# Two token tiles to an accumulator bank, weights loaded a job ahead, decay rows on ScalarE's queue

## The chip, the cores and the metric

The kernel runs on one core of a Trainium2 chip. The metric is the time of one execution on the device in microseconds (us), the median of several runs. A core has five engines with a queue of instructions each, worked through in order: TensorE (PE, matrix multiplications into PSUM banks), VectorE (DVE), ScalarE (ACT), GpSimd (POOL) and SyncE (SP, which here only starts transfers). ACT also starts transfers. PSUM banks of 128 x 512 floats hold what PE has summed until ACT or DVE has read it.

## What is computed

One decoder layer over 1024 tokens of width 1024 with two branches: differential attention (8 heads) and a Mamba-2 scan (8 groups of 4 heads). Cut to what matters:

```python
h = rmsnorm(x, g_pre)
q, k, v, g_att, z, xbc, dt_raw, merge_logits = jnp.split(h @ w_in, SPLIT_IDX, axis=-1)
# attention: two softmax maps for each head, a = p0 - lam * p1, causal, with a bias by distance
o = rmsnorm(diff_attention(q, k, v, rel_bias, lam), att_subln_g) * (1.0 - lambda_init)
y_att = (o * silu(g_att)) @ w_att_proj
# scan: depthwise convolution over 4 tokens, then chunks of tokens with a running state
xs, Bm, Cm = split(silu(causal_depthwise_conv(xbc, conv_w, conv_b)))
dt = softplus(dt_raw + dt_bias)
a_cs = cumsum(dt * -exp(a_log))                    # within a chunk
y_diag = einsum((Cm . Bm) * tril(exp(a_cs[l] - a_cs[s])), xs * dt)
y_off = einsum(Cm, state) * exp(a_cs)
state = state * exp(a_cs[-1]) + einsum(Bm, exp(a_cs[-1] - a_cs), xs * dt)
y = group_rmsnorm((y_diag + y_off + d_skip * xs) * silu(z), ssm_norm_g, 8)
y_ssm = y @ w_ssm_proj
mixed = sigmoid(gate_att) * y_att + sigmoid(gate_ssm) * y_ssm
x = x + rmsnorm(mixed @ w_out, g_post)
```

## The kernel before

All projections are split: an operand is a rounded high part plus a low part, and a product is three matmuls (`mm3`, L153). A weight arrives by a transfer on SP's queue (`load_cols`, L143) in a buffer `raw`, ACT rounds it (L97) and POOL or DVE subtracts (L98). Of `raw` there are three buffers, so SP's next load waits until a split is done.

The stages, in order of time: the **head** squares, scales and transposes x (`ptx`, L386) into hT as high and low parts (`hTH` L388 on ACT, `hTL` L389 on DVE); **attention** runs 8 heads; `pya` projects its output; the **groups** of the scan, eight of them with eight chunks each; the **final projections** `pys` (of the scan's output) and `pout`. For half of the tokens, `pys` is begun early within the last group (`pye`, read at L889).

A `Stream` holds jobs: keys, queries, values (`pv`) and a merge gate for a head; in a group four convolution channels b, c, x0, x1 (`pub`, `puc`, `pux`) and the gate z (`pz`). A job is a load and steps of 12 matmuls of 512 columns or 24 of 256. Between the score blocks of attention and the chunks of the scan a number of steps is taken. `pv` and `pz` have the tokens on the partitions: a tile of 128 tokens gives 128 x 256 in a bank of its own. All these go through two PSUM banks (`psp`). ACT takes a tanh of the bank (`sz`, L706), then DVE multiplies with the bank (L707); a convolution is read twice by ACT (L725, L726), then come three taps on DVE (L728), a tanh on ACT (L729) and a product on DVE (L730).

A chunk needs a tile `mt` of decays: the row of a_cs for 4 heads, broadcast to 128 partitions by a transfer from DRAM (`mt<-arow_d`, SP's queue, L752, four buffers, three chunks ahead), then four Relu and an Exp on ACT (L783, L784) and a product with `cbm` on DVE (L785). `prepare` (L755) makes the transposes `px`, copied by ACT into `xb` (L768); `advance` (L787) has the matmuls `pd` that use `mt` and the state, and `finish` (L817) norms four chunks, transposes (`pty`) and stores `yT` (L829, L830) in DRAM as y_d, from where `yT_l` comes back (L963) as the operand of `pys`.

PE's order is that of the code (`manual_schedule`, L251). The order on ACT, DVE, POOL and SP is made by a scheduler from the program order and the priorities (`high_priority`) that some instructions carry.

Of the kernel before, what the change touches and what calls it, by code (L numbers as in the profile page):

```python
# [46 lines left out]
AHEAD = 2000  # L47
# [27 lines left out]
def tile_hybrid_layer(ctx: ExitStack, tc: tile.TileContext, x, g_pre, w_in, lq1, lk1, lq2, lk2,  # L75
# [56 lines left out]
    def load_cols(w, row0, col0, width, tag, name, off=0, wh=None, wl=None, eng=None):  # L132
# [4 lines left out]
        for c in range(0, width - off, P):  # L137
            n = min(P, width - off - c)
            cols = slice(off + c, off + c + n)
            for k0 in range(0, KT, 4):  # L140
                raw = wts.tile([P, 4, P], F32, tag="raw", bufs=3, name=f"{name}r{off + c}_{k0}")
                r0 = row0 + k0 * P
                nc.sync.dma_start(raw[:, :, 0:n], w[r0:r0 + 4 * P, col0 + c:col0 + c + n].rearrange("(k p) c -> p k c", p=P))  # L143
                split(wh[:, k0:k0 + 4, cols], wl[:, k0:k0 + 4, cols], raw[:, :, 0:n], eng)
# [26 lines left out]
    def proj_N(w, t, n, name):  # L171

        wh, wl = w
        ps = psp.tile([P, 512], F32, tag="pp", name=name)
        sl = slice(t * P, (t + 1) * P)
        mm3(ps[:, 0:n], [((hTH[:, k, sl], hTL[:, k, sl]), (wh[:, k, 0:n], wl[:, k, 0:n])) for k in range(KT)])
        return ps

    class Stream:
# [5 lines left out]
        def add(self, load, steps):  # L185
            self.jobs.append([load, steps, None])

        def load(self, i):
            if i < len(self.jobs) and self.jobs[i][2] is None:
                self.jobs[i][2] = self.jobs[i][0]()  # L190

        def advance(self):

            if self.at is None:
                for i in range(self.ahead + 1):
                    self.load(self.done + i)
                self.at = self.jobs[self.done][1](self.jobs[self.done][2])
            try:
                next(self.at)
                return True  # L200
# [50 lines left out]
    pe_scope.enter_context(tc.manual_schedule(engines={mybir.EngineType.PE}))  # L251
# [10 lines left out]
    class Head:  # L262
# [15 lines left out]
        def keys(self, w, half):  # L278
# [3 lines left out]
            with tc.high_priority(offset=AHEAD):  # L282
                nc.scalar.activation(kh[lo, 0, sl], ps[lo], AF.Copy)
                nc.scalar.activation(kh[hi, 1, sl], ps[hi], AF.Copy)
                nc.vector.tensor_tensor(kl[lo, 0, sl], ps[lo], f32(kh[lo, 0, sl]), op=ALU.subtract)
                nc.vector.tensor_tensor(kl[hi, 1, sl], ps[hi], f32(kh[hi, 1, sl]), op=ALU.subtract)
            for part in (kh, kl):
                nc.scalar.dma_start(f32(part[hi, 0, sl]), f32(part[lo, 0, sl]))
                nc.scalar.dma_start(f32(part[lo, 1, sl]), f32(part[hi, 1, sl]))
            yield  # L290

        def queries(self, w, half):
# [3 lines left out]
            with tc.high_priority(offset=AHEAD):  # L296
                nc.scalar.activation(qs[lo, 0, sl], ps[lo], AF.Copy, scale=DK ** -0.5)
                nc.scalar.activation(qs[hi, 1, sl], ps[hi], AF.Copy, scale=DK ** -0.5)
                nc.vector.scalar_tensor_tensor(qs[hi, 0, sl], ps[lo], DK ** -0.5, f32(qs[lo, 0, sl]), op0=ALU.mult, op1=ALU.subtract)
                nc.vector.scalar_tensor_tensor(qs[lo, 1, sl], ps[hi], DK ** -0.5, f32(qs[hi, 1, sl]), op0=ALU.mult, op1=ALU.subtract)  # L300
            yield

        def load_values(self):
            wh = wts.tile([P, KT, 288], F32R, tag="wbh", bufs=1, name=f"wvh{self.h}")
            wl = wts.tile([P, KT, 288], F32R, tag="wbl", bufs=1, name=f"wvl{self.h}")
            load_cols(w_in, 0, OV + self.h * P, P, "", f"wv{self.h}", wh=wh, wl=wl, eng=nc.gpsimd)
            load_cols(w_in, 0, OG + self.h * P, 2 * P, "", f"wg{self.h}", off=P, wh=wh, wl=wl, eng=nc.gpsimd)
            return wh, wl

        def values(self, w):  # L310
            vv, gg = self.vv, self.gg
            for t in range(NT):
                ps = proj_N(w, t, 256, f"pv{self.h}_{t}")
                with tc.high_priority(offset=AHEAD):
                    nc.scalar.activation(vv[:, t, 0:DV], ps[:, 0:DV], AF.Copy)
# [767 lines left out]
```

## Time and profile before

| | |
|---|---|
| median of three runs | 1950.76 us (1948.28 to 1950.99) |
| the profiled execution | 1953.8 us, of which the span is 1951.9 |
| mean granted clock of PE | 0.978 |
| transfers | 175.64 MB, mean 90 GB/s |
| SP's wait at L752 for PE's pd | 264.0 us, 38 times, longest 15.5 |
| the chain that ended last | PE 35%, DVE 8%, DMA 6% (5% of it mt<-arow_d), ACT 3% |

A row of a timeline begins with the start and the duration in us, then the engine, the line, the operation, what it writes and what it reads, how often, and in brackets how long the engine had been idle and what ended that. In lists of waits the numbers are total, count and longest. A group of instructions of the same kind is given as total busy time and mean of one. Time at which an engine that holds nobody up is idle costs nothing.

### The profile page before, as it was taken

The numbers are of one execution on the slowest core, as the hardware profiler recorded it, in microseconds if no ns is written. First come the engines' busy times: TensorE is split into PE (matmuls) and PEld (weight loads), VectorE is DVE, ScalarE is ACT, GpSimd is POOL, SyncE is SP. The second block draws the span as 40 slices with busy tenths as digits, with TensorE's granted clock in tenths as the row PEclk, the third lists the DMA queues.
The fourth block names the chain that finished last, engine by engine and source line by source line (L and its number), as shares of the span: only waits on it lengthen the run. The fifth ranks groups of instructions, "written<-read, shape, count | busy, mean of one in ns | idle before, by whom it ended". The sixth has DMA issues, their size and how long they took to land.

```text
span 1951.9 us, 27895 instructions
## 1 busy us (share of the span) xinstructions
PE 1830.9 (94%) x10249; PEld 1579.8 (81%) x10249; DVE 1159.9 (59%) x2564; ACT 858.7 (44%) x2143; POOL 473.6 (24%) x388
## 2 busy tenths in 40 slices
PE   4999999999999999999989899999999988798998
PEld 3888988889889888888778787888888876576886
DVE  4265665655656553126756759686867778564333
ACT  5345454555545443115544446455544455242211
POOL 2212111121111112212422314142332325341210
PEclk9999999999999999999999999999999998898999
DMA  5322122131221126422222223232322234674422
GB/s 164 87 55 79 36 82 58 49 84 39 73 63 44 58 73 208 150 75 63 65 55 76 65 72 91 55 91 56 82 61 74 75 95 152 206 239 132 157 83 79
DMA packets 225734, 175.64 MB, mean 90 GB/s; under 512 B 13116, under 2 KB 187550, under 8 KB 225598
## 3 DMA queue, kind: packets, MB, share of 16 engines
q1 hardware_dynamic: 193660, 116.48, 21.8%
q10 hardware_dynamic: 31938, 57.38, 8.8%
q8 instruction: 81, 1.33, 0.3%
q14 instruction: 55, 0.45, 0.1%
HBM read 133.82 MB, written 33.17 MB: 86 GB/s over the span
## 4 chain that ended last, share of the span: by engine, by line
PE 35%; DVE 8%; DMA 6%; ACT 3%; issue 2%; POOL 1%; SPq 0%; ACTq 0%; DVEq 0%; POOLq 0%
PE pys L153 6%; PE pz L153 6%; DMA mt<-arow_d 5%; PE pout L153 5%; PE puc L153 4%; PE pub L153 4%; PE pux L153 3%; DVE xT L728 3%; PE pd L793 2%; PE pg L153 1%; ACT mt L783 1%; PE pd L796 1%; PE pd L798 1%; DVE rst_y L107 1%; PE pye L153 1%
## 5 line engine op out<-in xcount | busy, mean ns | idle before, releaser
L153 PE MATMUL pz<-wzh,hTH 128*128 128x256 f32 (+1 forms) x512 | 157.2, 307 | 39.5 <-ACT xT L726 21.8
L153 PE MATMUL pz<-wzl,hTH 128*128 128x256 f32 (+1 forms) x512 | 151.4, 296 | 0.0
L153 PE MATMUL pz<-wzh,hTL 128*128 128x256 f32 (+1 forms) x512 | 150.8, 295 | 0.0
L783 ACT ACTIVATE mt<-mt,acs 128x128 f32<-128x128 f32 x256 | 86.5, 392 | 141.7 <-DMA mt<-arow_d 129.5
L153 PE MATMUL pv<-wvl,hTH 128*128 128x256 f32 x512 | 144.5, 282 | 0.0
L153 PE MATMUL pv<-wvh,hTL 128*128 128x256 f32 x512 | 144.2, 282 | 0.0
L153 PE MATMUL pv<-wvh,hTH 128*128 128x256 f32 x512 | 143.4, 280 | 0.0
L153 PEld LDWEIGHTS pz<-wzh,hTH 128*128 128x128 f32 x512 | 103.0, 201 | 46.3 <-ACT xT L726 24.9
L779 POOL TENSOR_TENSOR v<-xb,dsk 128x256 f32<-128x256 f32 x64 | 53.2, 831 | 225.7 <-ACT xb L768 205.1
L153 PEld LDWEIGHTS pz<-wzl,hTH 128*128 128x128 f32 x512 | 103.0, 201 | 0.4
L153 PEld LDWEIGHTS pz<-wzh,hTL 128*128 128x128 f32 x512 | 102.5, 200 | 0.0
L153 PEld LDWEIGHTS pv<-wvh,hTH 128*128 128x128 f32 x512 | 97.2, 190 | 0.6 <-PE pq L153 0.6
L153 PEld LDWEIGHTS pv<-wvl,hTH 128*128 128x128 f32 x512 | 96.7, 189 | 0.0
L153 PEld LDWEIGHTS pv<-wvh,hTL 128*128 128x128 f32 x512 | 96.1, 188 | 0.0
L447 DVE TENSOR_REDUCE ng<-s 128x2 f32<-128x1024 f32 (+2 forms) x96 | 91.5, 954 | 1.8
L728 DVE SCALAR_TENSOR_TENSOR xT<-ux,cw,xT 128x512 f32<-128x512 f32 x96 | 85.2, 887 | 11.8 <-ACT xT L726 11.0
L98 DVE TENSOR_TENSOR al<-pta,ah 128x512 fp32r<-128x512 f32 (+2 forms) x96 | 51.0, 554 | 50.1 <-ACT ah L97 49.0
L458 ACT ACTIVATE p<-s,ngm 128x512 f32<-128x512 f32 (+3 forms) x128 | 76.0, 611 | 7.0 <-DVE ngm L453 6.4
L805 POOL TENSOR_TENSOR st<-st,elast 128x256 f32<-128x256 f32 x48 | 39.1, 815 | 141.1 <-DVE st L806 113.3
L793 PEld LDWEIGHTS pd<-xdt,mt 128*128 128x128 f32 x512 | 65.5, 196 | 8.7 <-DVE mt L785 5.1
L490 PE MATMUL po<-vv,al 128*128 128x256 f32 x288 | 72.2, 284 | 0.0
L793 PE MATMUL pd<-xdt,mt 128*128 128x64 f32 x512 | 66.0, 273 | 6.0 <-DVE mt L785 6.0
(1110 smaller groups left out, 5697.7 us busy)
## 6 DMA issues: line engine op xcount, KB each, us to landing
mt<-arow_d SPq DMA_DIRECT2D x64, 256.0 KB, 5.0
sig_d<-gt ACTq DMA_DIRECT2D x32, 256.0 KB, 2.0
y_d<-yT ACTq DMA_DIRECT2D x32, 256.0 KB, 2.9
yT_l<-y_d SPq DMA_DIRECT2D x24, 256.0 KB, 4.9
kh<-kh ACTq DMA_DIRECT2D x32, 128.0 KB, 2.2
kl<-kl ACTq DMA_DIRECT2D x32, 128.0 KB, 2.6
o_d<-oT ACTq DMA_DIRECT2D x16, 256.0 KB, 2.0
oTl<-o_d SPq DMA_DIRECT2D x8, 512.0 KB, 4.3
```

The costliest lines, as they stand in the source:

```text
L98: (eng or nc.vector).tensor_tensor(l, src, f32(h), op=ALU.subtract)
L107: nc.vector.scalar_tensor_tensor(t, t, -0.5, v, op0=ALU.mult, op1=ALU.mult)
L153: nc.tensor.matmul(ps, a, b, start=(i == 0), stop=(i == n - 1))
L447: nc.vector.tensor_reduce(ng, s[:, :, 0:width], axis=AX.X, op=ALU.max, negate=True)
L458: nc.scalar.activation(self.p[i][:, m, 0:width], s[:, m, 0:width], AF.Exp, bias=neg[:, m:m + 1], accum_out=sums[:, i, m:m + 1])
L490: nc.tensor.matmul(po[:, 0:256], al, vv[:, k, :], start=False, stop=(k == qb))
L728: nc.vector.scalar_tensor_tensor(out_h, u[:, j:j + 512], cw3[:, j, ct:ct + 1], out_h, op0=ALU.mult, op1=ALU.add)
L779: nc.gpsimd.tensor_tensor(v4(self.v), xs, b4(dsk[:, hs]), op=ALU.mult)
L783: nc.scalar.activation(mt[:, i, :], mt[:, i, :], AF.Relu, scale=-1.0, bias=acs[:, c, g.g * HG + i:g.g * HG + i + 1])
L793: nc.tensor.matmul(pd[:, 0, i * PH:(i + 1) * PH], mt[:, i, :], self.xdt[:, i * PH:(i + 1) * PH], start=True, stop=True)
L796: nc.tensor.matmul(pd[:, 1, 256:512], self.xb[:, 256:384], self.xe, start=True, stop=True)
L805: nc.gpsimd.tensor_tensor(v4(new), v4(state), b4(elast[:, c, hs]), op=ALU.mult)
```

## The change

The change keeps every matmul. It removes all priorities and instead delays what is emitted: `post(n, fn)` holds a piece of code back for n steps of the stream, `tick` counts a step and emits what is due, `flush` emits the rest. Splits of loaded weights, multiplications that follow a tanh, taps and tanh of the convolutions and the products of a chunk are posted so.

```diff
+    def post(n, fn):
+
+        item = [now[0] + n, fn]
+        posts.append(item)
+        return item
...
-                raw = wts.tile([P, 4, P], F32, tag="raw", bufs=3, name=f"{name}r{off + c}_{k0}")
...
+                    raw = wts.tile([P, 4, P], F32, tag="raw", bufs=4, name=f"{name}r{off + c}_{i}")
...
-                split(wh[:, k0:k0 + 4, cols], wl[:, k0:k0 + 4, cols], raw[:, :, 0:n], eng)
+                post(after + i, lambda raw=raw, i=i, n=n, cols=cols:
+                     split(wh[:, i * 4:i * 4 + 4, cols], wl[:, i * 4:i * 4 + 4, cols], raw[:, :, 0:n], eng or nc.gpsimd))
```

All jobs of heads and of groups are put in the stream beforehand, so that a job's weights are loaded one job ahead across the border of a head or a group. Values and gates z put two token tiles in a bank (except in the first group):

```diff
+            count = 1 if g == 0 else 2
+            for t in range(0, NT, count):
+                ps = psp.tile([P, 512], F32, tag="pp", name=f"pz{g}_{t}")
...
+                    proj_N(w, t, 256, ps[:, 0:256])
+                    yield
+                    proj_N(w, t + 1, 256, ps[:, 256:512])
+                z = ps[:, 0:256 * count].rearrange("p (t c) -> p t c", t=count)
+                sz = self.sz[:, t:t + count, :]
+                nc.scalar.activation(sz, z, AF.Tanh, scale=0.5)
...
+                    post(1, lambda sz=sz, z=z: nc.vector.scalar_tensor_tensor(sz, sz, 1.0, z, op0=ALU.add, op1=ALU.mult))
```

The load of `mt` goes to ACT's queue, its Relu and Exp get a function of their own that is called before `prepare`, the state's decay goes from POOL to DVE:

```diff
+        def decays(self):
+            g, c, mt = self.group, self.c, self.mt
+            for i in range(HG):
+                nc.scalar.activation(mt[:, i, :], mt[:, i, :], AF.Relu, scale=-1.0, bias=acs[:, c, g.g * HG + i:g.g * HG + i + 1])
+            nc.scalar.activation(mt, mt, AF.Exp, scale=-1.0)
...
-            nc.sync.dma_start(self.mt, bass.AP(arow_d.tensor, arow_d.offset + self.group.g * HG * S + self.c * P,
+            nc.scalar.dma_start(self.mt, bass.AP(arow_d.tensor, arow_d.offset + self.group.g * HG * S + self.c * P,
...
-                        nc.gpsimd.tensor_tensor(v4(new), v4(state), b4(elast[:, c, hs]), op=ALU.mult)
+                    nc.vector.tensor_tensor(v4(new), v4(state), b4(elast[:, c, hs]), op=ALU.mult)
```

In the other direction, the copies of keys and the small transfers th, mx, xr, gpost and mix_d go from ACT's queue to SP's. In the head, ACT squares all eight tiles in a row, DVE does all the scaling, transposes come in pairs and use two banks of the scores besides:

```diff
+        for t in range(NT):
+            squared(t)
+            if t == 3:
+                scaled(0)
+        turned(0, (0, 1))
...
+        turned(0, (6, 7))
+        scaled(1)
```

In attention the sum of the two maps' outputs is one reduction on DVE instead of a copy on ACT and a sum on DVE. In the scan, the z of the last group moves partly behind that group's first chunk, `pye` starts at its third chunk, the loads of w_out only at its fifth, and yT and ys have a buffer less each. Every second of the first eight y loads for `pys` is issued on ACT:

```diff
+            steps = 24 + 4 * (g in (0, 1)) - 4 * (g == SG - 2)
...
+            if (g, c) == (SG - 1, 2):
+                stream.finish(marks[SG])
...
-                nc.sync.dma_start(f32(tl), y_d[i, :, sl])
-                split(th, tl, f32(tl), nc.gpsimd if i % 2 else nc.vector)
+                (nc.scalar if half == 0 and i % 2 else nc.sync).dma_start(f32(tl), y_d[i, :, sl])
+                items.append(post(after, lambda i=i, th=th, tl=tl: split(th, tl, f32(tl), nc.gpsimd if i % 2 else nc.vector)))
```

What this makes of the order, at the places that matter. ACT in the middle of the scan, before, at the border of two groups (`sqy_7` squares the last chunk of the one, `mt_3` belongs to the fourth chunk of the next, L783 is Relu, L784 Exp, `xb` the copy of px; each sz is one token tile):

```order
L814 ACTIVATE sqy_7_12218,ssy_1_11564<-v_7_12012 128x256 [waits DVE_49,Pool_49]
L783 ACTIVATE mt_3_12390<-mt_3_12390,acs 128x128 [waits DMAHW1_49,PE_49]
L783 ACTIVATE mt_3_12390<-mt_3_12390,acs 128x128 x2
L706 ACTIVATE sz_12023<-pz_5_12238 128x256 [waits PE_49]
L783 ACTIVATE mt_3_12390<-mt_3_12390,acs 128x128
L768 ACTIVATE xb_1_12272<-px_1_12267 128x512 [waits PE_49]
L784 ACTIVATE mt_3_12390<-mt_3_12390 128x512 [waits Activation_49]
L706 ACTIVATE sz_12023<-pz_6_12288 128x256 [waits PE_49]
L706 ACTIVATE sz_12023<-pz_7_12315 128x256 [waits PE_49]
```

ACT at the same place after the change:

```order
L863 DMA mt_3_12191<-arow_d 128x4x128 [waits PE_49]
L926 ACTIVATE sqy_7_12062,ssy_1_11379<-v_7_11827 128x256 [waits DVE_49,Pool_49]
L858 ACTIVATE mt_3_12191<-mt_3_12191,acs 128x128 [waits DMAHW2_49]
L858 ACTIVATE mt_3_12191<-mt_3_12191,acs 128x128 x2
L795 ACTIVATE sz_11835<-pz_4_11996 128x512 [waits PE_49]
L878 ACTIVATE xb_1_12090<-px_1_12085 128x512 [waits PE_49]
L858 ACTIVATE mt_3_12191<-mt_3_12191,acs 128x128
L859 ACTIVATE mt_3_12191<-mt_3_12191 128x512 [waits Activation_49]
L795 ACTIVATE sz_11835<-pz_6_12096 128x512 [waits PE_49]
```

The trigger of the load of mt now stands on ACT itself, one instruction ahead of its first Relu, and a sz covers two token tiles.

ACT at the start, before (`sqx` squares a tile of x, `xt` scales one, `hTH` reads a transposed bank):

```order
L374 ACTIVATE sqx_3_151,ssx_144<-xt_113 128x1024 [waits DMAHW6_49,Activation_49]
L374 ACTIVATE sqx_0_228,ssx_227<-xt_118 128x1024 [waits DMAHW7_49,Activation_49]
L379 ACTIVATE xt_109<-xt_109,rsy_x_155 128x1024 [waits DVE_49]
L374 ACTIVATE sqx_1_230,ssx_227<-xt_120 128x1024 [waits DMAHW0_49,Activation_49]
L379 ACTIVATE xt_113<-xt_113,rsy_x_155 128x1024
L374 ACTIVATE sqx_2_232,ssx_227<-xs_qs 128x1024 [waits DMAHW1_49,Activation_49]
L97 ACTIVATE wk0h<-wk0r_0_126 128x512 [waits DMAHW3_49]
L374 ACTIVATE sqx_3_234,ssx_227<-xs_kh 128x1024 [waits DMAHW2_49,Activation_49]
L97 ACTIVATE wk0h<-wk0r_4_130 128x512 [waits DMAHW4_49]
L97 ACTIVATE wq0h<-wq0r_0_136 128x512 [waits DMAHW5_49]
L388 ACTIVATE hTH<-ptx_0_171,gcol 128x512 [waits PE_49]
L388 ACTIVATE hTH<-ptx_1_178,gcol 128x512 [waits PE_49]
```

And after:

```order
L424 ACTIVATE sqx_144,ssx_136<-xt_113 128x1024 [waits DMAHW6_49,Activation_49]
L424 ACTIVATE sqx_164,ssx_137<-xt_118 128x1024 [waits DMAHW7_49,Activation_49]
L424 ACTIVATE sqx_166,ssx_137<-xt_120 128x1024 [waits DMAHW0_49,Activation_49]
L424 ACTIVATE sqx_168,ssx_137<-xs_qs 128x1024 [waits DMAHW1_49,Activation_49]
L434 ACTIVATE hTH<-ptx_0_172,gcol 128x512 [waits PE_49]
L424 ACTIVATE sqx_170,ssx_137<-xs_kh 128x1024 [waits DMAHW2_49,Activation_49]
L434 ACTIVATE hTH<-ptx_1_173,gcol 128x512 [waits PE_49]
L97 ACTIVATE wk0h<-wk0r_0_126 128x512 [waits DMAHW3_49]
L97 ACTIVATE wq0h<-wq0r_0_132 128x512 [waits DMAHW5_49]
L434 ACTIVATE hTH<-ptx_2_190,gcol 128x512 [waits PE_49]
L97 ACTIVATE wk0h<-wk0r_1_128 128x512 [waits DMAHW4_49]
L97 ACTIVATE wq0h<-wq0r_1_134 128x512 [waits DMAHW6_49]
```

The squares of the second half no longer alternate with scalings, and the first hTH stands ahead of the splits of wk0 and of the last square.

SP between the early block and the final projections, after the change (`mix_d<-the` stores an early block, `yT_l<-y_d` loads the scan's output):

```order
L169 DMA wp_0_4r_0_16723<-in_w_ssm_proj 128x4x128 [waits DMAHW4_49,DMAHW1_49,Pool_49]
L1002 DMA mix_d<-the_16561 128x512 [waits DMAHW5_49,DMAHW2_49,DVE_49]
L1180 DMA gpost<-in_g_post 128x1024 [waits DMAHW3_49]
L1098 DMA yT_l_16605<-y_d 128x512 [waits PE_49]
L1098 DMA yT_l_16611<-y_d 128x512
L1098 DMA yT_l_16617<-y_d 128x512 [waits DMAHW0_49]
L1098 DMA yT_l_16623<-y_d 128x512 [waits DMAHW2_49]
L1121 DMA mx_0_16662<-mix_d 128x512 [waits DMAHW4_49,PE_49]
```

The y loads on SP stand behind the store of the last early block; four of the first eight are not here but on ACT's queue.

More of the change, by code (lines that the diff above doesn't have):

```diff
@@ L169, in proj_T, with proj_N @@
         return ps
[L171 removed]
+    def proj_N(w, t, n, ps):
         wh, wl = w
[L174 removed]
         sl = slice(t * P, (t + 1) * P)
[L176 to L177 removed]
+        mm3(ps, [((hTH[:, k, sl], hTL[:, k, sl]), (wh[:, k, 0:n], wl[:, k, 0:n])) for k in range(KT)])
     class Stream:
@@ L849, in tile_hybrid_layer @@
         chunks = [(g, c) for g in range(SG) for c in range(NT)]
-        made, squares = {}, {}
-        def chunk(i):
-            if i not in made:
-                g, c = chunks[i]
-                if c % 4 == 0:
-                    squares[g, c // 4] = small.tile([P, 4], F32, tag="ss4", name=f"ssy{g}_{c // 4}")
-                made[i] = Chunk(groups[g], c, squares[g, c // 4][:, c % 4:c % 4 + 1])
-            return made[i]
         early = []
```

581 lines of the change are left out of this document (339 added, 242 removed).

## The prediction

> **What bounds the kernel now.** I read the page's busy times first, then the windows by stage, then what TensorE (PE) waited for, and only then the queues behind those waits.
>
> ```profile
> PE 1830.9 (94%) x10249; PEld 1579.8 (81%) x10249; DVE 1159.9 (59%) x2564; ACT 858.7 (44%) x2143; POOL 473.6 (24%) x388
> 0.00:42.00 42.00, 17.38 (x77) 13.59 (x77) 19.46 (x44) 26.59 (x43) 10.27 (x12) 1.00 0.54 178
> 42.00:880.00 838.00, 823.36 (x4885) 721.61 (x4885) 438.65 (x1109) 368.00 (x1043) 143.05 (x108) 0.99 0.27 77
> 880.00:976.00 96.00, 91.95 (x422) 75.46 (x422) 70.44 (x114) 51.82 (x108) 31.68 (x26) 0.96 0.25 65
> 976.00:1561.60 585.60, 553.77 (x3257) 486.58 (x3256) 418.48 (x875) 287.24 (x682) 182.05 (x161) 0.98 0.27 71
> 1561.60:1709.50 147.90, 118.01 (x653) 100.26 (x651) 104.92 (x214) 66.18 (x156) 58.00 (x49) 0.91 0.50 154
> 1709.50:1951.90 242.40, 226.47 (x960) 182.33 (x960) 107.96 (x211) 58.90 (x115) 48.56 (x33) 0.96 0.42 136
> ```
>
> The columns of a window are its length, then busy time of PE, weight loads, DVE, ACT and POOL, then the granted clock. PE is busy 1830.9 of 1951.9 us, so 121 us of idle time is all that a new order can return, and besides it what the lowered clock costs inside "busy". The matmuls are the same in both kernels. By window (head; attention and its projection; the first group; six groups; last group and hand-over; final projections) the idle time is 24.6, 14.6, 4.1, 31.8, 29.9 and 15.9 us. One minus the clock, times the window, puts the clock's loss at about 0, 8, 4, 12, 13 and 10 us; over the six groups idle and clock together make 43.5. Attention has nearly nothing to give. The question is what holds PE in the other windows:
>
> ```profile
> PE pz L153 <- ACT xT L726: 21.8, 12, 4.0
> PE pz L153 <- DVE sz L707: 15.5, 12, 3.3
> PE ptx L386 <- DVE hTL L389: 14.5, 5, 7.1
> PE pys L153 <- ACT yT_h L97: 12.0, 1, 12.0
> ...
> PE pout L153 <- ACT mixH L1007: 6.2, 1, 6.2
> ```
>
> The numbers are total wait, count and longest. In the groups PE waits for a PSUM bank (pz after xT or sz): the evacuation is late. Why it is late, ACT and SP show:
>
> ```profile
> ACT mt L783 <- DMA mt<-arow_d: 104.7, 36, 6.2
> ACT ux L729 <- DVE xT L728: 55.0, 21, 6.0
> ACT sqy L814 <- DVE v L812: 37.2, 19, 5.2
> ACT ub L729 <- DVE bT L728: 16.7, 12, 2.1
> ACT uc L729 <- DVE cT L728: 10.1, 9, 2.3
> DMA to landing us min/median/max: 4.7/5.0/6.3
> ```
>
> The rows are of the six groups alone (976 to 1561.6); the last is the landing time of all 64 mt loads. ACT is busy only 287.24 of 585.6 us there, but it works in order: while it stands before a decay row that has not landed, the evacuation behind it stands too. One such place:
>
> ```profile
> 1097.88 0.39 PE L153 MATMUL pz<-wzh,hTH 128*128 128x256 f32 x1 [2.35 <-ACT xT L726]
> 1099.03 0.42 PE L153 MATMUL pz<-wzh,hTL 128*128 128x256 f32 x1
> 1102.02 0.36 PE L153 MATMUL pz<-wzl,hTH 128*128 128x256 f32 x1
> 1103.61 0.65 PE L796 MATMUL pd<-xe,xb 128*128 128x256 f32 x2
> 1105.38 0.27 PE L153 MATMUL pz<-wzl,hTH 128*128 128x256 f32 x1
> 1107.29 0.37 SPq L143 DMA_DIRECT2D wx03r<-in_w_in  x1
> 1107.75 0.46 SPq L752 DMA_DIRECT2D mt<-arow_d  x1
> 1107.97 0.28 PE L153 MATMUL pz<-wzh,hTL 128*128 128x256 f32 x1
> 1112.57 1.28 ACT L783 ACTIVATE mt<-mt,acs 128x128 f32<-128x128 f32 x4 [2.98 <-PE px L764]
> 1115.02 0.39 PE L153 MATMUL pz<-wzh,hTH 128*128 128x256 f32 x1 [2.48 <-DVE sz L707]
> ```
>
> The diagonal matmuls that last read the old mt buffer ended at about 1103.6, yet SP issued the new load at 1107.75, behind a weight load at 1107.29: 4.1 us lost in SP's order. With 5.0 us of landing that is 1112.75, about where ACT's Relu starts at 1112.57 (the trace names a transpose that ended then, too), and PE waited 2.48 us for the sz behind it. A 256-wide tile of 24 matmuls lasts 24 x 0.118 = 2.8 us at full clock (22 steps from 1105.38 to 1107.97), and that is all the time in which a single-tile bank can be emptied unseen.
>
> The clock: after the 2.35 us wait the 14 steps from 1099.03 to 1102.02 take 0.214 us each instead of 0.118, so this wait cost 14 x 0.096 = 1.3 us more. *The Trainium skill's "TensorE: Matmul & The Clock Gate", in "Why this matters for your kernels", says that the clock falls back only after gaps above about 3 us. The row differs, and it decides. By the page's rule waits of this length would return no clock, and the sum below would end 8 us higher.*
>
> **The change, part by part.** *Pairs (pz, pv).* Two tiles share a bank, so the time in which the previous bank can be emptied grows from 2.8 to 5.6 us. Against it, the multiplication that ends the bank (L707) is now posted one step, some 2.8 us, later. Of the 37.3 us in the two pz rows, whose longest waits are 4.0 and 3.3, the sz waits (mean 1.3) fit into what remains. The xT waits are half at the first z tile, which still waits for the evacuation two banks before, and half at the second, which goes. I count 15.5 + 11 = 26 us of waits, about 20 of them in the six groups. Two 256-wide activations become one 512-wide; that saves ACT and DVE some tenths of a us per pair, off the path, and I cost it at nothing.
>
> *Decay rows on ACT's queue.* SP's 4.1 us go. But the load is now triggered by an engine that works in order, and it stands 0 to 2 instructions ahead of its own Relu in five of eight chunks of a group, and 3 to 7 ahead in the others. From the 5.0 us landing I estimate 4 us of exposure in five chunks and 1.3 in three: 24 us of ACT's time per group, where the before row has 104.7 / 6 = 17.5. What stands behind it are the xb copy, sz and the conv evacuations, for which PE waits. ACT's list for a group is then 287.24/6 = 47.9 busy, 24 for mt, 55.0/6 = 9.2 for ux, (16.7 + 10.1)/6 = 4.5 for ub and uc, 37.2/6 = 6.2 for sqy: 91.8 us. A dense PE needs 97.6 - 43.5/6 = 90.4 us. The two are nearly level. So I do not take the whole 43.5 us but **26 us** for the six groups (20 of waits and 6 of clock): 93.3 us a group, 1.5 above ACT's list. Bounds: 43.5 from the dense PE; on the other side minus 47, with ACT at 105.4 us a group (the slower rival). *The Trainium skill's "DMA: Bandwidth & Descriptors", in "Issuing engines are not separate DMA queues", says that another issuing engine saves only the sequencer's time to start a DMA. The issue takes 0.46 us in the row at 1107.75, but the row also shows 4.1 us of waiting in the queue, which the sentence leaves out. By it the move gives nothing and ACT loses, which is the limited rival below.* The first group keeps single tiles: **1 us** of its 8, bounds 0 and 4.
>
> *Head.*
>
> ```profile
> 12.08 1.42 DVE L381 TENSOR_SCALAR xt<-xt,rsy_x 128x1024 f32<-128x1024 f32 x2
> 23.81 1.97 PE L386 MATMUL ptx<-cst,xt 128*128 128x128 f32 x8 [7.12 <-DVE hTL L389]
> 31.76 0.78 PE L153 MATMUL pk<-hTH,wk0h 128*128 128x512 f32 x1
> 23.01 0.74 DVE L389 SCALAR_TENSOR_TENSOR hTL<-ptx,gcol,hTH 128x512 fp32r<-128x512 f32 x1
> ```
>
> Between 15 and 24 us the second half's squares and square root stand ahead of the first half's hTH and hTL. In the new order ACT squares all eight tiles in a row, so that the first hTH comes at about 15 us; DVE scales four tiles (4 x 0.71 from 12.08, until 14.9), and the second half's square root is put behind the first half's pieces. Eight hTL at 0.74 and two extra banks then carry the first keys to about 21 us instead of 31.76. I take **11 us**; bounds 3 (ACT still has weight splits between) and 14.5 (the whole row of ptx after hTL).
>
> *Attention and its projection.* PE's order is the same, 823.36 of 838 us are busy. The key copies now stand on SP's queue behind weight loads, but are used 17 us later at the earliest (two 5.6 us keys or queries and four value tiles). **0**, bounds -8 and +5.
>
> *Last group and hand-over.*
>
> ```profile
> 1704.22 5.17 SPq L963 DMA_DIRECT2D yT_l<-y_d  x8
> 1709.46 0.80 PE L153 MATMUL pys<-yT_h,wp_0h 128*128 128x512 f32 x1 [12.01 <-ACT yT_h L97]
> y_d<-yT ACTq DMA_DIRECT2D x32, 256.0 KB, 2.9
> yT_l<-y_d SPq DMA_DIRECT2D x24, 256.0 KB, 4.9
> ```
>
> Four z tiles (4 x 2.8 = 11 us of PE work) move behind the first chunk of group 7, whose chunks had too little to fill them: 17.9 us of idle time beside the 12.0, and 13 of clock. I take 16 of these 31, bounds 2 and 27. At the hand-over two weight loads on SP stood ahead of the eight y loads, which were issued at 1704.22; half of these now go on ACT's queue. But yT has one buffer instead of two, so the chain from the last transpose is a yT (0.7), its store (2.9), the second yT and store (3.6), the load (4.9) and the split (0.6): 12.7 us, of which 24 early matmuls of 0.23 cover 5.6. With a queue's issue time that leaves about 8 of the 12 us: **4**, bounds 0 and 7. Together **20**, bounds 2 and 34.
>
> *Final projections.*
>
> ```profile
> 1757.36 0.40 PE L153 MATMUL pout<-woH,mixH 128*128 128x512 f32 x1
> 1758.99 0.39 PE L153 MATMUL pout<-woL,mixH 128*128 128x512 f32 x1
> 1943.54 0.69 DVE L1024 TENSOR_TENSOR yo<-pout,gpost 128x512 f32<-128x512 f32 x1 [4.92 <-PE pout L153]
> 1947.37 1.41 DVE L1034 SCALAR_TENSOR_TENSOR yo<-yo,rsy_e,xr 128x512 f32<-128x512 f32 x2
> out<-yo SPq DMA_DIRECT2D x16, 256.0 KB, 3.4
> ```
>
> Of the 6.2 us wait for mixH most stays: in the new order of ACT five y splits and two weight splits stand ahead of the last mixH, before seven and one. ys has one buffer less: from its first write (1943.54) to its store's landing (1948.78 + 3.4) 8.6 us pass, and PE takes 2 x 24 x 0.233 (the 7 steps from 1757.36 to 1758.99) = 11.2 us for the two banks of a block, so this costs nothing. The tail after the last matmul stays. **2**, bounds -4 and 10.
>
> Sum: 11 + 0 + 1 + 26 + 20 + 2 = 60 us. The profiled execution took 1953.8 us (span 1951.9 and 1.9 around it), 3.0 above the median of 1950.8: 1953.8 - 60 - 3.0 = **1891 us**.
>
> **The rivals.** *Limited: ACT sets the pace.* If each chunk exposes 3.7 us instead of 3.0, ACT's list is 67.8 + 8 x 3.7 = 97.4 us, and all seven later groups keep their time; the waits only change their names, pz on the late multiplication among them. What remains is the head, hand-over and final part: 11 + 4 + 2 = 17, so 1934 us. For it speaks that ACT's mt wait gets longer by the order; against it, that 55.0 us of ux waits lie partly under the same PE stalls and shrink with them.
>
> *Slower: every decay row exposed.* If the trigger comes right ahead of its Relu in all chunks, 4.7 us each (the 5.0 landing less one short instruction), ACT's list is 67.8 + 37.6 = 105.4 us, 7.8 longer than now, in seven groups 55; less 17 that is 38, so 1989 us. It decides from 4.1 us of exposure a chunk: 67.8 + 8 x 4.1 = 100.6, which is 3.0 above 97.6, in seven groups 21, and outweighs the 17 by 4. The order has longer gaps in three of eight chunks, so I give it little.
>
> *All returns.* Head 14.5, groups 43.5, first group 4, last group and hand-over 34, end 10: 106 us, 1845. It needs ACT's waits to hide entirely.
>
> *No visible change.* Several small gains are given back in the attention stage by SP's longer queue: 1951.
>
> **How the numbers follow.** Forecast 0.48 (1870 to 1912), limited 0.25 (1912 to 1947), all returns 0.13 (below 1870), no change 0.04, slower 0.10. A difference of 0.2% is about what a measurement here can tell from no change. Faster 0.86, same 0.04, slower 0.10. The range 1843 to 1946 leaves out the slower cases, no change, and the far end of the best one.
>
> **What would show it.** Right: pk begins near 21 us; pz waits for xT and sz fall under 15 us in all; the groups last near 93 us; the wait ahead of the first pys is near 8 us; ACT's wait for mt in the six groups is near 144 us (6 x 24) instead of 104.7. Wrong: groups at 97 us with px, pd or conv matmuls waiting for ACT (the limited case); an mt wait above 4 us a chunk (slower); or PE waits in the attention stage, where I cost nothing.

## The result and the profile after

The changed kernel takes 1892.85 us (median of four runs, 1885.8 to 1895.26) against 1950.88: a ratio of 0.9699, 95% interval 0.967 to 0.9727. The forecast was 1891. The profiled execution took 1895.26 us, its span is 1893.1. The total was met, its parts were not. Both profiles can be cut at the same matmuls of PE's order, since the work between two cuts is the same:

| from, to (first matmul of each) | before | after | gain | forecast |
|---|---|---|---|---|
| start, pk | 31.8 | 20.0 | 11.8 | 11 |
| pk, pya (attention) | 722.9 | 723.2 | -0.3 | 0 for both |
| pya, pz (its projection) | 88.8 | 96.1 | -7.3 | |
| pz, pd of the first group | 93.0 | 88.8 | 4.2 | 1 |
| pd of the first, pd of the seventh group | 582.2 | 540.3 | 41.9 | 26 |
| pd of the seventh group, pys | 190.8 | 185.4 | 5.4 | 20 |
| pys, end | 242.4 | 239.3 | 3.1 | 2 |
| sum | 1951.9 | 1893.1 | 58.8 | 60 |

The windows of both kernels, in columns as in the prediction (behind the granted clock stand the busy share of the DMA engines and the GB/s that they moved); before, the projection and the six groups, then after, the same two and the two pieces behind them:

```profile
754.70:843.50 88.80, 87.72 (x386) 71.93 (x385) 15.35 (x20) 14.56 (x26) 26.95 (x20) 1.00 0.49 150
936.50:1518.70 582.20, 550.37 (x3227) 483.80 (x3228) 418.32 (x873) 285.22 (x678) 183.14 (x161) 0.97 0.27 70
```

```profile
743.20:839.30 96.10, 91.45 (x385) 73.29 (x386) 22.75 (x21) 17.90 (x28) 36.43 (x23) 0.96 0.51 164
...
928.10:1468.40 540.30, 532.09 (x3226) 472.35 (x3227) 408.65 (x885) 285.79 (x658) 153.50 (x126) 0.99 0.29 76
1468.40:1552.30 83.90, 76.99 (x438) 66.79 (x437) 66.92 (x134) 46.32 (x108) 25.91 (x20) 0.96 0.36 104
1552.30:1653.80 101.50, 81.26 (x436) 67.73 (x434) 71.55 (x146) 42.95 (x94) 41.32 (x33) 0.91 0.58 176
```

In the six groups the idle time fell from 31.8 to 8.2 us, that is 23.6, and PE's busy time for the same 3226 matmuls fell by 18.3. Some 11 of these are the clock. In the kernel before it was granted at 0.50 in seven stretches of 3.4 or 6.8 us, 29 us of the six groups; after the change one such stretch of 7 us is left, at their start. Two of the seven, then the six groups after the change in two pieces:

```profile
996.40:1003.20 6.80, 6.04 (x28) 6.04 (x29) 4.14 (x11) 1.79 (x5) 0.85 (x1) 0.50 0.14 39
1098.80:1102.20 3.40, 3.40 (x18) 3.40 (x17) 3.37 (x8) 1.67 (x4) 1.34 (x2) 0.50 0.02 5
```

```profile
928.10:936.10 8.00, 7.00 (x22) 5.62 (x23) 6.46 (x12) 2.18 (x5) 3.61 (x3) 0.57 0.35 97
936.10:1468.40 532.30, 525.09 (x3205) 466.73 (x3204) 402.19 (x873) 283.61 (x654) 149.89 (x123) 1.00 0.29 75
```

A stretch at half clock loses half its length: (29 - 7) / 2 = 11. The other 7 us are not the clock. Outside such stretches the 512-wide convolution matmuls follow each other by 0.227 us after the change and by 0.232 before (medians), which for some 1190 of them makes 4 to 6 us. The kernels b1, b2 and b4 below have 0.232 and e1 and e2 have 0.227, so this came with another part of the change; which part, no run shows.

Over the last group and the hand-over idle and busy time fell by only 2.7 us each. PE's waits after, in the whole run:

```profile
PE pys L180 <- ACT yT_h L97: 11.3, 2, 10.9
PE ptx L447 <- DVE xt L430: 7.0, 4, 6.4
...
PE px L872 <- DVE xT L823: 6.0, 1, 6.0
PE pz L180 <- ACT xT L816: 5.1, 4, 1.4
PE pout L180 <- ACT mixH L1133: 4.5, 1, 4.5
PE pty L941 <- DVE v L936: 4.3, 4, 2.1
...
PE pya L180 <- POOL oTl L98: 3.3, 4, 1.3
```

The bank waits of pz have gone from 37.3 us to 8.6 (this row and two of sz with 3.5). The wait ahead of the first pys has stayed, 10.9 after 12.0. New are px after xT (transposes that wait for the last convolution) and the row of pya. ACT's waits after, in the six groups:

```profile
ACT mt L858 <- DMA mt<-arow_d: 74.3, 31, 5.0
ACT sqy L926 <- DVE v L923: 50.9, 23, 4.8
ACT ux L825 <- DVE xT L820: 32.4, 12, 4.4
```

The prediction had expected 144 us in the first row; it fell from 104.7 to 74.3.

### The profile page after: what moved, and what is told of

The parts are those of the page before. It is cut to its first block, busy times and chain, and to the rows that moved or that the text cites. A ratio compares the mean times of both kernels' runs of the same rounds, so it can differ in the third digit from the quotient of the medians.

```text
span 1893.1 us, 27752 instructions
## 1 busy us (share of the span) xinstructions
PE 1803.6 (95%) x10249; PEld 1566.7 (83%) x10249; DVE 1161.9 (61%) x2584; ACT 828.1 (44%) x1983; POOL 441.5 (23%) x344
## 4 chain that ended last, share of the span: by engine, by line
PE 29%; DVE 10%; DMA 8%; ACT 5%; issue 2%; POOL 1%; SPq 0%; ACTq 0%; DVEq 0%; POOLq 0%
PE pz L180 8%; PE pys L180 5%; PE pout L180 5%; DMA mt<-arow_d 3%; PE pub L180 3%; DVE xT L820 2%; PE pux L180 2%; PE puc L180 1%; PE pd L905 1%; DVE cT L820 1%; PE pg L180 1%; DVE bT L820 1%; ACT mt L858 1%; DMA yT_l<-y_d 1%; PE pd L908 1%
## 5 line engine op out<-in xcount | busy, mean ns | idle before, releaser
L180 PE MATMUL pz<-wzh,hTH 128*128 128x256 f32 (+1 forms) x512 | 150.1, 293 | 8.6 <-ACT xT L816 5.1
L180 PE MATMUL pz<-wzl,hTH 128*128 128x256 f32 (+1 forms) x512 | 145.8, 285 | 0.0
L180 PE MATMUL pz<-wzh,hTL 128*128 128x256 f32 (+1 forms) x512 | 145.0, 283 | 0.0
L890 POOL TENSOR_TENSOR v<-xb,dsk 128x256 f32<-128x256 f32 x64 | 63.0, 985 | 297.5 <-ACT xb L878 253.7
L180 PEld LDWEIGHTS pz<-wzh,hTH 128*128 128x128 f32 x512 | 97.5, 190 | 10.5 <-ACT xT L816 5.9
L180 PEld LDWEIGHTS pz<-wzl,hTH 128*128 128x128 f32 x512 | 97.2, 190 | 0.5
L180 PEld LDWEIGHTS pz<-wzh,hTL 128*128 128x128 f32 x512 | 96.7, 189 | 0.0
L820 DVE SCALAR_TENSOR_TENSOR xT<-ux,cw,xT 128x512 f32<-128x512 f32 x96 | 81.7, 851 | 11.5 <-ACT xT L816 10.2
L568 PE MATMUL po<-vv,ah 128*128 128x256 f32 x288 | 71.4, 282 | 0.0
L512 PE MATMUL s<-kh,qs 128*128 128x512 f32 (+2 forms) x192 | 70.3, 374 | 0.0
```

The costliest lines, as they stand in the source:

```text
L180: nc.tensor.matmul(ps, a, b, start=(i == 0), stop=(i == n - 1))
L512: nc.tensor.matmul(s[:, m, 0:wide], head.qs[:, m, qsl], head.kh[:, m, l0:l0 + wide], start=True, stop=False)
L568: nc.tensor.matmul(po[:, 0:256], ah, vv[:, k, :], start=(k == 0), stop=False)
L820: nc.vector.scalar_tensor_tensor(out_h, u[:, j:j + 512], cw3[:, j, ct:ct + 1], out_h, op0=ALU.mult, op1=ALU.add)
L890: nc.gpsimd.tensor_tensor(v4(self.v), xs, b4(dsk[:, hs]), op=ALU.mult)
```

## The experiments

Each kernel was timed in several rounds beside the kernel before. "Groups" below is the stage from the first pd of the first group to that of the seventh, "last group" the one from there to the first pys. Where an edit doesn't touch them, the groups lie between 537.6 and 540.3 us and the last group between 183.1 and 186.2 in the profiles, so a difference of 5 us in a stage can be read even where the totals' intervals touch.

### One part of the change alone, in the kernel before

**b1_pairs_z**: z in pairs for groups 1 to 7, all else as before.

```diff
-            for t in range(NT):
-                ps = proj_N(w, t, zw, f"pz{g}_{t}")
+            count = 1 if g == 0 else 2
+            for t in range(0, NT, count):
+                ps = psp.tile([P, 512], F32, tag="pp", name=f"pz{g}_{t}")
...
+                    proj_N(w, t, 256, ps[:, 0:256])
+                    yield
+                    proj_N(w, t + 1, 256, ps[:, 256:512])
...
```

> The kernel before with one edit: the gate z has two token tiles to a bank in groups 1 to 7. Stage from the first pd of the first group to the first pd of the seventh: 582.2 us before. Theory P (pairs give the slack): 20 to 30 us shorter, and PE's pz waits of 29.7 us there fall below 10. Rival (the waits are ACT's lateness, which pairs only move to other matmuls): 0 to 8 us shorter.

1916.84 us, ratio 0.9818 (0.9795 to 0.9842). Groups 554.5, 27.7 shorter; last group 183.0, 7.8 shorter. PE's and ACT's waits in its groups:

```profile
PE pz L153 <- DVE sz L715: 5.3, 3, 3.5
PE pz L153 <- ACT xT L734: 5.2, 5, 2.4
```

```profile
ACT mt L791 <- DMA mt<-arow_d: 102.2, 34, 7.0
```

ACT waits for mt as long as ever, and PE hardly feels it: 29.7 us of pz waits became 10.5, where theory P had them below 10. That is theory P. That ACT and DVE have fewer and longer instructions is no rival: it saves them only 1.4 and 4.7 us of busy time in these groups.

**b2_mt_on_act**: the load of mt on ACT's queue.

```diff
-            nc.sync.dma_start(self.mt, bass.AP(
+            nc.scalar.dma_start(self.mt, bass.AP(
...
```

> The kernel before with one edit: the loads of mt start on ACT's queue. ACT's wait for mt in the six groups was 104.7 us. Theory A (a trigger on ACT lengthens ACT's waits): above 120, the stage of 582.2 us the same or up to 20 longer. Theory B (SP's queue held the loads back): below 85, the stage 5 to 20 us shorter.

1935.17 us, ratio 0.9912 (0.9885 to 0.994). Groups 570.5, 11.7 shorter. In its groups:

```profile
ACT mt L783 <- DMA mt<-arow_d: 78.7, 32, 5.1
ACT sqy L814 <- DVE v L812: 46.5, 29, 5.4
ACT ux L729 <- DVE xT L728: 28.7, 12, 6.0
```

Theory A, the prediction's, falls: with the trigger on ACT the wait for mt is 26 us shorter, and the wait for the taps of the convolution (ux) halves, from 55.0. Theory B's numbers are met, but the reason that it gives is not in the traces. In the kernel before, SP was ready for 32 of the 48 loads of these groups and stood waiting until PE's pd had freed the buffer:

```profile
SPq L752 <- PE pd L793: 220.9, 32, 15.5
```

From the end of that pd to the issue of the load 1.0 us passed on average on SP, and 1.8 us with this edit on ACT. So the loads start no earlier on average, and still ACT waits less. With the edit the scheduler also gave ACT another order (some 100 of its 678 instructions in these groups stand elsewhere), and no run separates the two.

**b3_head_order**: no priority for the second half's squares and square root.

```diff
-        with tc.high_priority(offset=AHEAD):
-            scaled(1)
+        scaled(1)
```

> The kernel before with one edit: the second half's squares and square root in the head have no priority any more. The first pk started at 31.76 us before and at 20.01 after the change. If the place of the second half's square root on DVE was the loss: pk at 22 to 26 and the whole kernel 5 to 9 us faster. If the extra banks and DVE's scaling are what matters (rival): pk at 29 to 32, no difference.

1947.06 us, ratio 0.9978 (0.996 to 0.9997). The first pk starts at 27.37 instead of 31.76, between the two expectations: the place of the square root is 4.4 of the 11.8 us; the other edits in the head were not taken apart.

**b4_all_three**: the three edits together.

> The kernel before with the three edits together: z in pairs, mt on ACT's queue, no priority in the head. If the three carry the change's gain in the head and the groups (11.75 and 41.9 us): 35 to 50 us faster in all. If the posted products and splits and the new places of the decays carry half of it (rival): 15 to 30 us faster.

1900.06 us, ratio 0.973 (0.9708 to 0.9752): 53 us, above what was expected of it. Alone the three gave 36, 18 and 6, so they nearly add, and together they are some nine tenths of the change's gain. Groups 547.7, last group 179.4, which is 6 us better than in the change itself. PE's idle time in the groups is 8.5 us, with the whole change 8.2: the posted splits and products took next to no waits from PE there, and the 7 us between the two kernels are busy time.

### One part of the change undone

**e1_mt_on_sp**: the reverse of b2's edit, in the changed kernel.

> The changed kernel with one edit: the loads of mt start on SP's queue again. Stage measured: from the first pd of the first group to the first pd of the seventh (582.2 us before, 540.3 after the change); ACT's wait for mt there was 104.7 us before and 74.3 after. Theory A (the prediction's: a trigger on ACT lengthens ACT's waits): the mt wait falls below 70 and the stage is the same or up to 10 us shorter. Theory B (SP's queue held the loads back behind weight loads, and that was the loss): the mt wait rises above 100 and the stage is 10 to 30 us longer, 550 to 570.

1920.76 us, ratio 0.9842 (0.9817 to 0.9867). Groups 564.6, 24 longer:

```profile
ACT mt L858 <- DMA mt<-arow_d: 95.1, 32, 6.1
ACT ux L825 <- DVE xT L820: 62.0, 22, 4.8
```

```profile
PE pux L180 <- ACT xT L816: 9.8, 5, 3.0
PE pz L180 <- DVE sz L800: 9.3, 6, 4.6
```

The stage is theory B's, and the price is higher than in the kernel before; the mt wait, 95.1, stays below the 100 that B had named. Again the loads do not start later on SP (1.8 us after the pd on average, 2.1 on ACT). The taps' wait (ux) rises more than that of mt, from 32.4 to 62.0. Why was not tried.

**e2_single_z**: z single again, its multiplication at once.

```diff
-            count = 1 if g == 0 else 2
+            count = 1
...
-                    post(1, lambda sz=sz, z=z: nc.vector.scalar_tensor_tensor(sz, sz, 1.0, z, op0=ALU.add, op1=ALU.mult))
+                    nc.vector.scalar_tensor_tensor(sz, sz, 1.0, z, op0=ALU.add, op1=ALU.mult)
```

> The changed kernel with one edit: the gate z has one token tile to a bank again, in all groups, and its multiplication is not posted a step later. Stage from the first pd of the first group to the first pd of the seventh, 540.3 after the change. Theory P (the pairs give the slack that hides ACT's lateness): 20 to 35 us longer, and PE's waits of pz for xT and sz, 6.8 us now, are back above 20. Rival C (ACT is on time without them, by the new order of mt, taps and products): less than 8 us longer and pz waits below 12.

1921.22 us, ratio 0.9845 (0.9822 to 0.9868). Groups 562.6, 22 longer, pz waits 14.1 and 6.9: theory P again. Pairs and queue each give what the other can't: undoing either one alone gives back 22 to 24 of the 41.9 us.

**e4_z_before_last**: all z of the last group ahead of its first chunk.

```diff
-                    steps = 24 + 4 * (g in (0, 1)) - 4 * (g == SG - 2)
+                    steps = 24 + 4 * (g in (0, 1))
...
-            active = steps / NT if g + 1 < SG else 2 if c < 2 else 10 / 6
+            active = steps / NT if g + 1 < SG else 0 if c < 2 else 10 / 6
...
-            elif c == NT - 1 and g + 2 < SG:
+            elif c == NT - 1:
```

> The changed kernel with one edit: all of the last group's z tiles come before its first chunk again, and its first two chunks take no steps. From the first pd of the seventh group to the first pys: 190.8 us before the change, 185.4 after. If the prediction's step is right (the moved z tiles fill idle time of the last group): 8 to 16 us longer, 193 to 201. Rival (what holds PE there are weight loads and products that come late whatever PE does in between): 183 to 190.

1886.72 us, ratio 0.9674 (0.9657 to 0.9692). Last group 179.4: 6 us shorter than with the change, where the step of the prediction wanted 8 to 16 longer. The moved tiles did harm. What PE waits for in that stage in the changed kernel, and then in this one:

```profile
PE pys L180 <- ACT yT_h L97: 10.9, 1, 10.9
PE px L872 <- DVE xT L823: 6.0, 1, 6.0
PE pty L941 <- DVE v L936: 4.3, 4, 2.1
PE pye L180 <- ACT we5h L97: 2.8, 1, 2.8
```

```profile
PE pys L180 <- ACT yT_h L97: 11.1, 1, 11.1
PE pty L941 <- ACT woH L97: 2.3, 1, 2.3
PE pye L180 <- ACT we6h L97: 2.3, 1, 2.3
```

The wait of 6.0 us is gone. In the changed kernel it stands here:

```profile
1530.60 0.39 PE L180 MATMUL pux<-hTH,wu_7l 128*128 128x512 f32 x1
1530.83 0.27 PE L872 MATMUL px<-cst,xT 128*128 128x128 f32 x1
1537.14 0.47 PE L872 MATMUL px<-cst,xT 128*128 128x128 f32 x1 [6.05 <-DVE xT L823]
```

With the z tiles moved behind the group's border nothing is left for PE between the last convolution and the transposes of its result, and taps, tanh and product stand open. ACT's wait for mt in that stage fell from 27.4 to 10.3 us, too.

**e3_ol_on_dve**: the low parts of the attention output all on DVE.

```diff
-            split(th, tl, f32(tl), nc.gpsimd if i % 2 else nc.vector)
+            split(th, tl, f32(tl), nc.vector)
```

> The changed kernel with one edit: the low parts of the attention output (oTl) are all made by DVE, as before the change, not every second one by POOL. Stage from the first pya to the first pz: 88.8 us before, 96.1 after the change. If POOL's 3.2 us for one of them holds the first pya: 89 to 92 and the whole kernel 4 to 7 us faster. If the late start of ACT's splits is all of it (rival): 94 to 97, no difference in the total.

1888.52 us, ratio 0.9681 (0.9657 to 0.9704). From pya to pz 94.0 instead of 96.1, the lower edge of the rival's 94 to 97. The 2.1 us are the edit's all the same, since e1, e2, e4 and f2, which leave this stage alone, have 96.1 too. The total is 4.3 us lower with intervals that overlap. The larger part was elsewhere.

**f1_wpa_on_pool**: the same, and the second and third weight of the projection on POOL's queue.

```diff
-                nc.sync.dma_start(raw[:, :, 0:n], w[r0:r0 + 4 * P,
+                (q or nc.sync).dma_start(raw[:, :, 0:n], w[r0:r0 + 4 * P,
...
+                return *load_cols(w_att, 0, d * P, P, "wa", f"wpa{d}", q=nc.gpsimd if d in (1, 2) else None), ths
...
-            split(th, tl, f32(tl), nc.gpsimd if i % 2 else nc.vector)
+            split(th, tl, f32(tl), nc.vector)
```

> The changed kernel with two edits: the loads of the second and third weights of the attention's projection start on POOL's queue instead of SP's, and all oTl splits are on DVE. In the changed kernel SP stood 11 us before the third weight's load until a raw buffer came free, with the loads of the attention output behind it (issued from 733.26, though the last attention output products ended about 14 us earlier than before). Theory Q (weights loaded a job ahead held SP's queue): the first oTl is issued 8 to 13 us earlier and the stage from the first pya to the first pz, 96.1 us (94.0 with DVE splits alone), falls to 88 to 91. Rival (the loads wait for the buffers of the attention stage): issue and stage as with DVE splits alone, 93 to 95.

1886.98 us, ratio 0.967 (0.9645 to 0.9694). The place in the changed kernel, SP's queue and PE:

```profile
717.51 2.37 SPq L169 DMA_DIRECT2D wpa1r<-in_w_att_proj  x2
731.21 1.62 SPq L169 DMA_DIRECT2D wpa2r<-in_w_att_proj  x2
733.26 13.00 SPq L650 DMA_DIRECT2D oTl<-o_d  x8
743.18 0.50 PE L180 MATMUL pya<-oTh,wpa0h 128*128 128x512 f32 x1 [2.50 <-ACT oTh L97]
```

In this kernel:

```profile
724.02 15.47 SPq L650 DMA_DIRECT2D oTl<-o_d  x7
```

The loads start 9.2 us earlier and the stage is 91.8 us: 4.3 of the 7.3 lost us are back, 2.1 of them by DVE. Theory Q holds for the queue; its stage was put slightly too low (88 to 91). The 2.5 us wait for the first oTh is still there, since ACT does a gate's tanh and two weight splits ahead of it. It ends with the first pya, so it lies ahead of the stage, but the clock behind it is in the stage. In this kernel, as in the changed one, a stretch of 6.8 us at half clock follows that wait:

```profile
743.33:753.00 9.67, 8.40 (x23) 5.58 (x23) 9.59 (x8) 6.55 (x7) 0.56 (x1) 0.67 0.66 218
```

The loss is 0.33 x 9.67 = 3.2 us, about the 3 that have not come back.

### The hand-over, and the parts together

**f2_y_loads_first**: a priority for the y loads.

```diff
-                (nc.scalar if half == 0 and i % 2 else nc.sync).dma_start(f32(tl), y_d[i, :, sl])
+                if half == 0:
+                    with tc.high_priority(offset=2000):
+                        (nc.scalar if i % 2 else nc.sync).dma_start(f32(tl), y_d[i, :, sl])
+                else:
+                    nc.sync.dma_start(f32(tl), y_d[i, :, sl])
```

> The changed kernel with one edit: the eight y loads for the first pys carry a priority, so that SP's four stand ahead of the last early block's store and ACT's four ahead of three weight splits. The wait ahead of the first pys was 10.9 us. Theory H (it is SP's and ACT's order behind the last early block): 6 to 8 us, first pd of the seventh group to first pys 181 to 183 instead of 185.4. Rival (the landing of 6.4 us is contention of transfers, and an earlier issue only moves it): 10 to 11 us.

1886.22 us, ratio 0.9668 (0.9644 to 0.9691). The wait ahead of pys is 12.0 us, the last group 184.4: theory H falls. The rise itself says little, since this wait is 10.6 to 14.6 us in e1 to e4 and f1, which leave it alone. The y loads did pass the last early block's store, but not the weights:

```profile
1642.84 0.37 SPq L169 DMA_DIRECT2D wp_4r<-in_w_ssm_proj  x1
1643.30 2.57 SPq L1100 DMA_DIRECT2D yT_l<-y_d  x4
1649.98 0.32 SPq L1002 DMA_DIRECT2D mix_d<-the  x1
```

In ACT's queue the first split of a y load followed at 1649.95, 6.7 us behind the issue. What this kernel gained stands behind the first pys: from there to the end it takes 233.3 us, and 236.4 to 239.3 in the changed kernel and those that leave the y loads alone. Why was not tried.

**f3_together**: f1, f2 and e4 in one kernel.

> The changed kernel with the edits of four runs together: oTl splits on DVE and two weights on POOL's queue, y loads with priority, and the last group's z before its first chunk. If the parts add: 7 us in the attention's projection, 3 at the hand-over, 6 in the last group, so 1876 to 1880 beside 1893. If they overlap: 1882 to 1888.

1878.0 us (1876.17 to 1880.61), ratio 0.9627 (0.9597 to 0.9657), clear of the change's 0.967 to 0.9727 and the fastest of all. In the total most of it adds: e4, f1 and f2 alone are 6.1, 5.9 and 6.6 us below the change, all together 14.9. By stage it did not come as expected. The projection (91.9) gave 4.2 us instead of 7, the last group with the hand-over in it (178.8) 6.6 instead of 9, though the wait ahead of pys fell to 8.3; 3.5 came behind the first pys, and 2.5 in the six groups, which no edit touches.

**f4_wp_on_pool**: f3 and the first weights of the final projection on POOL's queue.

```diff
+                q = nc.gpsimd if ds[0] in (1, 3) else None
+                ws = [load_tail(D, d, f"wp1_0_{d}", q) for d in ds[-1:]]
...
```

> The four edits together (1878.0 us) and one more: the loads of the weights one to four of the first half's final projection start on POOL's queue, so that SP has none of them ahead of its y loads (one, waiting for a raw buffer, stood there until 1634.06, and PE had ended its early blocks at 1632.2). Theory Q (weights a job ahead in SP's queue hold the y loads): issue within 1 us of the last early matmul, the wait ahead of the first pys 8.3 falls to 6 to 7 us, 1874 to 1877 in all. Rival (what is left is the landing of the y loads, 4.6 to 6.4 us, and a split): 8 to 9 us, no difference.

1893.36 us, ratio 0.9722 (0.9705 to 0.9738): both expectations missed in the total, 15 us slower than f3. SP was free now and issued the y loads at 1632.35, 0.7 us before PE's last early matmul ended. The wait ahead of the first pys is 9.1 us even so, near the rival's 8 to 9. And POOL works in order as well:

```profile
1653.69 0.75 POOL L169 DMA_DIRECT2D wp_3r<-in_w_ssm_proj  x1 [5.93 <-DMA yT_l<-y_d]
1654.46 1.28 POOL L98 TENSOR_TENSOR yT_l<-yT_l,yT_h 128x512 fp32r<-128x512 f32 x1
1655.79 0.80 PE L180 MATMUL pys<-yT_l,wp_0h 128*128 128x512 f32 x1 [11.36 <-POOL yT_l L98]
```

It stood before a weight load, with the low part of y behind it that PE waited 11.36 us for, most of the 12.4 us between the two spans. The same move that paid for mt on ACT costs here, because an operand of the next matmul was queued behind it.

## Why the prediction was right, and where it was not

**The total was right by two terms that were off in opposite directions.** The six groups gave 41.9 instead of 26 us, the last group with the hand-over 5.4 instead of 20. That the two cancel to 2 us of the forecast is luck.

*Pairs.* Right, and shown from both sides (b1, e2): the added slack takes up ACT's lateness. The waits were put at 20 us in the groups, the idle time fell by 23.6.

*The clock.* The step that was mis-sized in the groups: "20 of waits and 6 of clock". Measured were 23.6 of waits, 11 of clock and 7 of other busy time, mostly a shorter step between matmuls, that stood in no term. The clock's whole loss in these groups was read nearly right, 12 us where the seven stretches make 14.5; the step that failed was to expect half of it back. That the gain came near the bound of 43.5 with 8 us of idle time left is the shorter step's doing. Five of the seven stretches came with single waits of 2.35 to 2.7 us. The Trainium skill's "TensorE: Matmul & The Clock Gate" ("Why this matters for your kernels") has the clock fall after gaps above about 3 us; by that little would have come back, and the runs decide against it.

*Decay rows on ACT's queue.* The time was right in sign, the reason wrong. "24 us of ACT's time per group" was worked out from how many instructions stand between the trigger and its Relu. It is 74.3 / 6 = 12.4. What stands between them waits as well: sqy, for DVE, whose wait rose to 50.9 us. That this wait runs beside the landing is read from the order and not shown by a run. Summed like the prediction's, ACT's list is 78 us a group instead of 91.8, and a group takes 90: ACT was not level with a dense PE, and the limited and the slower rival had no ground. The move was worth 18 us alone (b2) and 28 when undone (e1), but not by the 4.1 us in SP's order: that row is one of 13 among 48 loads that came over 1 us after the pd, and on ACT they come later still. What shortened ACT's waits stays open, with ACT's new order as the nearest rival. None of these waits was urgent: before the change ACT ran the first Relu of a row 36 us or more ahead of the pd that uses it. The Trainium skill's "DMA: Bandwidth & Descriptors" ("Issuing engines are not separate DMA queues") counts only the time to start a transfer as saved; here 18 to 28 us were saved, though the loads started no earlier on average.

*Head.* Right, 11.8 for 11; the square root's place is 4.4 of it (b3). The gain in pk's start is kept: pya comes 11.5 us earlier. The lead-in to the first group gave 4.2 for 1, the final projections 3.1 for 2; neither was taken apart.

*Attention and its projection, at nothing.* Attention itself was, at -0.3. The projection lost 7.3 us, near the end of the bound of -8, by what the prediction had looked for only in the key copies: weights a job ahead stood in SP's queue before the attention output (f1), and POOL's share of the splits (e3). The 3 us that are left are about the clock's loss behind PE's wait for the first oTh. That wait itself, 2.5 us, is new and stands in attention's row.

*Last group: "Four z tiles ... move behind the first chunk" for 16 us.* Failed; the sign was wrong. The 5.4 us came from pairs and queue, which alone give 7.8 and 5.2 there (b1, b2) and with the head's order 11.4 (b4), and the moved tiles took 6 back (e4). The idle time that they were to fill was not what the end of the group waited for, and they had been the cover of the last convolution.

*Hand-over: 12 to 8.* It stayed at 10.9. The chain of the second yT and its store, on which the 8 was built, is not in this path: the first pys need only the first half of the tokens, whose last store was issued at 1608.96, 37 us ahead of these loads. What stands there are the loads: 3.3 us from PE's end until SP issues them, and then 7.6 to the first pys. An earlier issue alone did not end it (f4: 9.1 us). Why their landing takes 6.4 us (median of SP's) instead of 4.9 was not tried.

## What to carry to other kernels

A wait on an engine that works in order costs what is queued behind it, so a transfer belongs on the queue where the least urgent work follows: moving weight loads onto an engine that still owed PE an operand cost 15 us here. Moving one load from SP's queue to ACT's was worth 18 to 28 us, but the load started no earlier for it on average, so a queue that looks crowded is not yet the reason. An accumulator that holds twice the work buys slack against all such lateness at once, without removing any of it. When a total comes out as forecast, cut both traces at the same matmuls: here one stage had given 16 us more than thought and another 15 less, and the part that had done harm could be taken out again.

## What was not expected of the hardware

Waits of PE of less than 3 us can bring its clock down. In the six groups of the kernel before, eight waits of PE were 2.35 us or longer, up to 4.0, and seven of them came with a stretch of 3.4 or 6.8 us at half clock; none of the shorter waits did. No sharp length follows from it: in b2, e1 and e2 waits of 2.0 to 2.2 us came with such a stretch, and one of 3.1 us in e2 did not. The 1.7 us that a stretch of 3.4 loses is two thirds of such a wait again, while the waits of about 1 us cost only themselves.

And DVE and POOL slow each other in the same kind of subtraction. In the changed kernel four on POOL and three on DVE ran side by side; the last row is e3, where DVE did all eight and six came in a row:

```profile
744.15 12.87 POOL L98 TENSOR_TENSOR oTl<-oTl,oTh 128x1024 fp32r<-128x1024 f32 x4 [0.39 <-ACT oTh L97]
743.16 1.68 DVE L98 TENSOR_TENSOR oTl<-oTl,oTh 128x1024 fp32r<-128x1024 f32 x1 [14.68 <-ACT oTh L97]
745.05 9.75 DVE L98 TENSOR_TENSOR oTl<-oTl,oTh 128x1024 fp32r<-128x1024 f32 x3 [0.21 <-ACT oTh L97]
...
743.31 7.48 DVE L98 TENSOR_TENSOR oTl<-oTl,oTh 128x1024 fp32r<-128x1024 f32 x6 [14.68 <-ACT oTh L97]
```

DVE's took 3.25 us each beside POOL's 3.2, 1.68 when mostly alone and 1.2 in e3. POOL had none of this size alone; its subtractions of half the size take 1.29 us alone, so 2.6 is an estimate for it. Sharing them between the two engines gained nothing: with all on DVE the stage is 2.1 us shorter.
